# The second block's down projection by Strassen's scheme: seven products of halves, and PSUM banks that are read in the middle of a sum

## The chip, the cores and the metric

The kernel runs on one core of a Trainium2 chip. The metric is the device time of one execution in microseconds, the median of several runs. In one core TensorE (PE in the profile, PEld its weight loads) multiplies, VectorE (DVE) and ScalarE (ACT) work element by element and can read PSUM, the eight banks into which TensorE accumulates, GpSimd (POOL) works element by element on SBUF, and SyncE (SP) starts most of the DMA transfers.

## The reference, cut to what matters

512 tokens of width 1024 go through a first block (a mixer with three branches, cross-attention, a convolutional feed-forward layer) and a second one (two kinds of attention, an output projection, a feed-forward layer). Only the second feed-forward layer bears on the change; its weights are `w_ff1_2` (1024 x 4096) and `w_ff2_2` (4096 x 1024):

```python
D_MODEL, SEQ = 1024, 512
D_FF = 4 * D_MODEL
...
        x = x + merged @ w_out[l]
        h = rms_norm_2(x, g_mlp[l])
        x = x + jnp.square(jax.nn.relu(h @ w_ff1[l])) @ w_ff2[l]
    return rms_norm_2(x, g_final)
```

## The kernel before, in words

**Numbers.** Every fp32 operand of a matrix product is split in two: `h`, a copy rounded to fp32r (ScalarE), and `l`, the rest (VectorE, `l = x - h`). A product is then three matmuls, h·h, h·l and l·h (`mm3`), summed in one PSUM bank. A weight piece is 256 rows by 512 columns or 1024 rows by 128 columns, 512 KB: a DMA brings it into `wr` (four buffers), ScalarE writes `wh` and VectorE `wl` (in this layer four buffers of each, two in the pool `w` and two more in `w_mlp`).

**The layer.** `ffn_relu2` takes the 4096 hidden features in four passes of 1024. In a pass, `gemm_f` (up) makes eight tiles of 128 features by 512 tokens: each is 8 steps of the sum times three matmuls of 512 columns into one bank. `ev_up` takes the bank out as relu times itself into `r` (L468, L469) and splits it into `ah` and `al`. Then `gemm_w` (down) takes two column halves of 512 outputs; for each, four banks hold the four groups of 128 tokens (t), and four weight pieces pass by, each used by all four t: per pass 2 halves x 4 t x 8 steps x 3 matmuls, all of 512 columns. The banks are added to the residual `h` in SBUF (`add_to`, L1527). In the last pass and half, `hold=3` keeps three pieces back, so that the four t end one after the other; `Residual.ev` adds the bank (L346), squares and sums the row on ScalarE (L271), and `step` runs the final norm of the rows behind it: `scale` on GpSimd (L279, L366, L371), `row` on VectorE into `xnt` and a DMA to the output (L387, L389).

**Before the layer.** The output projection (`mh`, `ml` in the pool `mh2`) ends with another `Residual` (`n_mlp`), whose `row` writes `xnt` and whose `turn` transposes it on TensorE into the layer's input `xh`, `xl`. The first two up tiles of the layer run in halves of 256 tokens, so that they can begin before the last two groups of tokens are there.

**Order.** The framework puts in the waits, and it sets the order of the instructions on each engine when the program is built: the context is opened with `schedule_with_timeline_sim=True`, so the order on an engine is one of planned times and not that of the code. On the chip an engine then keeps that order. A tile's buffer is given to the next tile of its name when all that read it are done.

Of the kernel before, what the change touches and what calls it, by code (L numbers as in the profile page):

```python
# [88 lines left out]
class Core:  # L89
# [58 lines left out]
    def wpiece(self, *srcs, pool=False):  # L148
# [9 lines left out]
        for s in srcs:  # L158
            self.nc.sync.dma_start(raw[:, :, c:c + s.shape[1]], s.rearrange("(k p) n -> p k n", p=128))
            c += s.shape[1]  # L160
        self.wi = (self.wi + 1) % (2 + self.wmore)
        p = self.wp if self.wi < 2 else self.wx
# [14 lines left out]

    def mm3(self, out, lh, ll, rh, rl, first, last):
        mm = self.nc.tensor.matmul
        mm(out, lh, rh, start=first, stop=False)  # L180
        mm(out, lh, rl, start=False, stop=False)  # L181
        mm(out, ll, rh, start=False, stop=last)  # L182

# [56 lines left out]
    def gemm_w(self, src, nk, n, xh, xl, evac, hold=1):  # L240
# [10 lines left out]
        for c0 in range(0, n, 512):  # L251
# [9 lines left out]
            for t in range(nt):  # L261
# [3 lines left out]
                yield  # L265


    def sumsq(self, src, ss, out=None):
# [61 lines left out]
class Residual:  # L330
# [3 lines left out]

    def __init__(self, core, pool, h, g, g2=None, dst=None):
        self.core, self.pool, self.h, self.dst = core, pool, h, dst
        self.gb = core.bcast(pool, g, D, "gb")
        self.gb2 = None if g2 is None else core.bcast(pool, g2, D, "gb2")
        self.ss = pool.tile([128, NT, 2, 2], F32, name="rss")
        self.sq = pool.tile([128, 512], mybir.dt.bfloat16, name="rsq")  # L340
        self.wait, self.rs = {}, {}

    def ev(self, t, c0, w, ps):
# [4 lines left out]
        if self.gb2 is not None:  # L348
            nc.gpsimd.tensor_tensor(x, x, self.gb[:, c0:c0 + w], op=ALU.mult)
            self.core.sumsq(x, self.ss[:, t, 1, c0 // 512:c0 // 512 + 1], self.sq)  # L350
        if c0 + w == D:
            self.step(t)

    def step(self, t):
# [18 lines left out]
    def row(self, t):  # L373
# [4 lines left out]
        h, rs = self.h[:, t], self.rs[t]  # L378
        y = self.pool.tile([128, D], F32, name="xnt", bufs=2)
        out = None if self.dst is None else self.dst[t * 128:(t + 1) * 128]  # L380
# [75 lines left out]


def ffn_relu2(core, pool, h, xh, xl, up, down, mid, res):
    nc = core.nc
    nf = down.shape[0] // 128  # L460
    for f0 in range(0, nf, 8):
        n = min(8, nf - f0)
        ah = pool.tile([128, 8, T], F32R, name="ah", bufs=2)
        al = pool.tile([128, 8, T], F32R, name="al", bufs=2)

        def ev_up(m, ps):
            r = pool.tile([128, T], F32, name="r", bufs=3)
            nc.scalar.activation(r, ps, AF.Relu)  # L468
            nc.vector.tensor_tensor(r, ps, r, op=ALU.mult)  # L469
            core.split(ah[:, m], al[:, m], r)  # L470

        yield from core.gemm_f(up[:, f0 * 128:(f0 + n) * 128], 8, n * 128, xh, xl, ev_up, mid if f0 == 0 else None, wide=True)

        yield from core.gemm_w(down[f0 * 128:(f0 + n) * 128], n, D, ah[:, 0:n], al[:, 0:n], *((add_to(core, h),) if f0 + n < nf else (res.ev, 3)))

# [1229 lines left out]
def second_block(core, I, out):  # L1705
# [4 lines left out]
    with ExitStack() as right:  # L1710
# [39 lines left out]
        hp = core.hp.enter_context(core.pool("h2"))  # L1750
        h = hp.tile([128, NT, D], F32, name="h")
        n_mlp = ExitStack()
        with core.weights(1, "w_out2", 2), core.pool("mh2") as p:
# [3 lines left out]
            right.close()  # L1757
            res = Residual(core, n_mlp.enter_context(core.pool("n_mlp", side=1)), h, I["g_mlp_2"])
            drain(core.gemm_w(I["w_out_2"], 8, D, mh, ml, res.ev, 2))
    with core.weights(2, "w_mlp"), core.pool("mlp") as p:  # L1760
        last = Residual(core, p, h, I["g_final_2"], dst=out)

        def mid():
            res.rest()
            n_mlp.close()

        drain(ffn_relu2(core, p, h, *res.x, I["w_ff1_2"], I["w_ff2_2"], mid, last))
        last.rest()
# [46 lines left out]
```

## Time and profile before

| what | value |
|---|---|
| median of 3 runs | 2014.29 us (2011.59 to 2017.02) |
| the profiled execution's own time | 2016.94 us |
| its span, first to last instruction | 2015.1 us |
| TensorE busy | 1958.1 us of the span, 10844 matmuls |
| VectorE busy | 1115.8 us |
| ScalarE busy | 850.8 us |
| granted TensorE clock, mean | 0.983 of full speed |

Busy times are sums of recorded durations. Matmuls overlap in the pipeline, so the record of one (0.39 us) is longer than the distance to the next. The profiled execution took 2.65 us more than the median of the runs; 1.84 us of it lie outside the span.

### The profile page before, as it was taken

The page shows a single profiled execution, that of the slowest core. Times are in us where ns is not written, and L with a number is a line of the kernel's source. Part 1 is how long each engine was busy: PE and PEld are TensorE (multiplying, and loading weights), DVE is VectorE, ACT ScalarE, POOL GpSimd, SP SyncE. Part 2 cuts the span into 40 slices and gives each one's busy share as a digit, 9 for nine tenths or more (in the row PEclk, how much of TensorE's full clock was granted, in tenths as well). Part 3 has the DMA queues.
Part 4 walks back from the last instruction along what each step waited for, and adds up shares of the span by engine and source line. Part 5 has one row for each costly group of instructions (what it writes and reads, how often), then busy time and mean ns, then how long its engine had stood idle before and what let it go on. Part 6 is the DMA issues. An engine that isn't in the chain of part 4 may idle for free.

```text
span 2015.1 us, 27841 instructions
## 1 busy us (share of the span) xinstructions
PE 1958.1 (97%) x10844; PEld 1642.5 (82%) x10844; DVE 1115.8 (55%) x1835; ACT 850.8 (42%) x1474; POOL 321.5 (16%) x367
## 2 busy tenths in 40 slices
PE   7999999999899999999999998999999999999998
PEld 6777888888778988888888877888888878888886
DVE  4457353418965645465454547657889754343343
ACT  4433223335624443343342446567776433233232
POOL 1334123443320100200000021002344020000000
PEclk9999989999999999999999998999999999999999
DMA  6223223342365641333333326442222533333331
GB/s 170 74 68 81 74 76 100 105 151 63 106 226 161 192 125 43 97 104 97 100 96 94 94 87 202 129 126 74 64 80 89 188 105 94 96 96 102 94 94 53
DMA packets 280727, 215.01 MB, mean 107 GB/s; under 512 B 28206, under 2 KB 239812, under 8 KB 280468
## 3 DMA queue, kind: packets, MB, share of 16 engines
q1 hardware_dynamic: 261364, 205.23, 33.9%
q10 hardware_dynamic: 19232, 8.02, 1.6%
q8 instruction: 85, 1.39, 0.3%
q14 instruction: 46, 0.38, 0.1%
HBM read 195.35 MB, written 20.48 MB: 107 GB/s over the span
## 4 chain that ended last, share of the span: by engine, by line
PE 88%; DVE 6%; ACT 2%; issue 2%; POOL 1%; DMA 1%; SPq 1%; ACTq 0%; DVEq 0%; POOLq 0%
PE g L180 17%; PE g L181 16%; PE g L182 16%; PE s L180 9%; PE s L182 9%; PE s L181 9%; PE s L608 1%; PE s L622 1%; PE s L304 1%; PE p L891 1%; DVE sbr L692 1%; PE s L596 1%; PE s L595 1%; DVE ptl L172 1%; DMA wr<-in_ca_wkv_dram 1%
## 5 line engine op out<-in xcount | busy, mean ns | idle before, releaser
L164 ACT ACTIVATE wh<-wr 128x1024 fp32r<-128x1024 f32 x307 | 323.6, 1056 | 585.7 <-PE g L181 192.4
L165 DVE TENSOR_TENSOR wl<-wr,wh 128x1024 fp32r<-128x1024 f32 (+1 forms) x240 | 295.0, 1231 | 417.0 <-ACT wh L164 413.1
L180 PE MATMUL g<-xh,wh 128*128 128x512 f32 (+1 forms) x1168 | 454.7, 391 | 6.1 <-DVE rkr L782 2.4
L181 PE MATMUL g<-xl,wh 128*128 128x512 f32 (+1 forms) x1168 | 452.2, 388 | 2.2 <-DVE xl L172 2.1
L182 PE MATMUL g<-xh,wl 128*128 128x512 f32 (+1 forms) x1168 | 451.1, 387 | 0.0
L180 PEld LDWEIGHTS g<-xh,wh 128*128 128x128 f32 x1168 | 225.2, 193 | 50.9 <-issue 3.7
L181 PEld LDWEIGHTS g<-xl,wh 128*128 128x128 f32 x1168 | 225.4, 193 | 44.0 <-DVE xl L172 3.2
L182 PEld LDWEIGHTS g<-xh,wl 128*128 128x128 f32 x1168 | 225.1, 193 | 42.8 <-DVE wl L165 1.0
L165 POOL TENSOR_TENSOR wl<-wr,wh 128x1024 fp32r<-128x1024 f32 x67 | 169.3, 2530 | 425.3 <-ACT wh L164 410.6
L182 PE MATMUL s<-wh,al 128*128 128x512 f32 x324 | 127.1, 392 | 0.0
L181 PE MATMUL s<-wl,ah 128*128 128x512 f32 x324 | 127.1, 392 | 0.0
L180 PE MATMUL s<-wh,ah 128*128 128x512 f32 x324 | 127.0, 392 | 0.0
L181 PE MATMUL s<-xl,wh 128*128 128x512 f32 x288 | 112.9, 392 | 0.0
L180 PE MATMUL s<-xh,wh 128*128 128x512 f32 x288 | 112.8, 392 | 0.0
L182 PE MATMUL s<-xh,wl 128*128 128x512 f32 x288 | 112.8, 392 | 0.0
L279 POOL TENSOR_TENSOR ss<-rss 128x1 f32<-128x1 f32 (+1 forms) x20 | 6.8, 341 | 468.9 <-ACT rsq L271 468.9
L1122 POOL TENSOR_SCALAR sy<-sy,rsm,ngate 128x128 f32<-128x128 f32 (+1 forms) x64 | 42.5, 666 | 198.5 <-DVE rsm L1120 182.9
L172 DVE TENSOR_TENSOR ptl<-s,pth 128x256 fp32r<-128x256 f32 (+3 forms) x144 | 66.7, 475 | 12.1 <-ACT pth L171 11.2
L181 PEld LDWEIGHTS s<-wl,ah 128*128 128x128 f32 x324 | 60.8, 188 | 14.0
L180 PEld LDWEIGHTS s<-wh,ah 128*128 128x128 f32 x324 | 60.8, 188 | 13.9
L182 PEld LDWEIGHTS s<-wh,al 128*128 128x128 f32 x324 | 60.8, 188 | 14.0
L1118 ACT ACTIVATE sy<-sy,m 128x128 f32<-128x128 f32 (+1 forms) x96 | 53.7, 560 | 39.1 <-DVE m L1116 36.9
(491 smaller groups left out, 3690.7 us busy)
## 6 DMA issues: line engine op xcount, KB each, us to landing
wr<-in_w_ff_dram SPq DMA_DIRECT2D x64, 512.0 KB
wr<-in_w_comb_dram SPq DMA_DIRECT2D x62, 512.0 KB
wr<-in_ffn_up_dram SPq DMA_DIRECT2D x44, 512.0 KB
wr<-in_w_in_dram SPq DMA_DIRECT2D x36, 512.0 KB
wr<-in_ffn_down_dram SPq DMA_DIRECT2D x22, 512.0 KB
wr<-in_ca_wkv_dram SPq DMA_DIRECT2D x16, 512.0 KB
d_gate<-ff SPq DMA_DIRECT2D x24, 256.0 KB
gi<-d_gate SPq DMA_DIRECT2D x24, 256.0 KB
```

Source lines behind the costliest of these rows:

```text
L164: self.nc.scalar.activation(h, raw, AF.Copy)
L165: (self.nc.gpsimd if pool or self.lpool else self.nc.vector).tensor_tensor(l, raw, h.bitcast(F32), op=ALU.subtract)
L172: nc.vector.tensor_tensor(l, src, h.bitcast(F32), op=ALU.subtract)
L180: mm(out, lh, rh, start=first, stop=False)
L181: mm(out, lh, rl, start=False, stop=False)
L182: mm(out, ll, rh, start=False, stop=last)
L304: nc.tensor.transpose(ps[:, j * 128:(j + 1) * 128], x[:, j * 128:(j + 1) * 128], self.ident)
L595: mm(s, q[:, qs], kk[0][:, 0:n], start=True, stop=False)
L596: mm(s, q[:, qs], kk[1][:, 0:n], start=False, stop=last)
L608: core.nc.tensor.transpose(ps[:, c], p[:, c], core.ident)
L1118: nc.scalar.activation(y, y, AF.Exp, scale=-1.0, bias=m, accum_out=sm)
L1122: nc.gpsimd.tensor_scalar(y, y, scalar1=rs, scalar2=fac, op0=ALU.mult, op1=ALU.mult)
```

## The change

The hidden activations A of a pass (512 tokens x 1024 features) are cut into four quarters of 256 tokens x 512 features, the down weights B (1024 x 1024) into four quarters of 512 x 512, and the product is made from seven products of quarters or of their sums and differences (the form with fifteen additions, after Strassen and Winograd). A class `Halves` makes S3 = A11 - A21, S1 = A21 + A22, S2 = S1 - A11 and S4 = A12 - S2 beside A11, A12 and A22 as the up tiles come out of PSUM, and splits all of them. `gemm_s` loads B's quarters into `ws` (left columns) and `wr` (right columns), subtracts quarters in place on VectorE (`less`), splits each for its product, and runs the products. Two pairs of banks, `b1` and `b2`, are read into `h` and then added to by a later product (`more=True` leaves out the framework's check of groups). The normed rows `xnt` of both norms now lie in `ws` in place of two buffers of their own, and `Residual.ev` counts columns to see when a row is full. Blank lines are left out:

```diff
--- before.py
+++ after.py
@@ -158,6 +158,15 @@
         for s in srcs:
             self.nc.sync.dma_start(raw[:, :, c:c + s.shape[1]], s.rearrange("(k p) n -> p k n", p=128))
             c += s.shape[1]
+        return self.wsplit(raw, pool)
+    def wsplit(self, raw, pool=False):
+        k, n = raw.shape[1:]
+        def view(t):
+            return t[:, 0:k * n].rearrange("p (k n) -> p k n", k=k)
         self.wi = (self.wi + 1) % (2 + self.wmore)
         p = self.wp if self.wi < 2 else self.wx
         h, l = (view(p.tile([128, 1024], F32R, name=x)) for x in ("wh", "wl"))
@@ -175,11 +184,14 @@
             nc.vector.scalar_tensor_tensor(l, src, scale, h.bitcast(F32), op0=ALU.mult, op1=ALU.subtract)
-    def mm3(self, out, lh, ll, rh, rl, first, last):
-        mm = self.nc.tensor.matmul
-        mm(out, lh, rh, start=first, stop=False)
-        mm(out, lh, rl, start=False, stop=False)
-        mm(out, ll, rh, start=False, stop=last)
+    def mm3(self, out, lh, ll, rh, rl, first, last, more=False):
+        def mm(l, r, start, stop):
+            self.nc.tensor.matmul(out, l, r, start=start, stop=stop, skip_group_check=more)
+        mm(lh, rh, first, False)
+        mm(lh, rl, False, False)
+        mm(ll, rh, False, last)
     def gemm_f(self, src, nk, n, xh, xl, evac, halves=None, pieces=(), wide=False):
@@ -264,6 +276,68 @@
                 evac(t, c0, 512, pss[t])
                 yield
+    def gemm_s(self, src, ops, evac):
+        nc = self.nc
+        K = src.shape[0] // 2
+        cuts = [(k, min(2, K // 128 - k)) for k in range(0, K // 128, 2)]
+        own = {}
+        def load(i, j):
+            own[i, j] = []
+            for k, m in cuts:
+                p, name = (self.ws, "ws") if j == 0 else (self.wp, "wr")
+                t = p.tile([128, 1024], F32, name=name, bufs=4)[:, 0:m * 512].rearrange("p (k n) -> p k n", k=m)
+                r0 = i * K + k * 128
+                nc.sync.dma_start(t, src[r0:r0 + m * 128, j * 512:j * 512 + 512].rearrange("(k p) n -> p k n", p=128))
+                own[i, j].append(t)
+        def less(dst, a, b):
+            for d, x, y in zip(own[dst], own[a], own[b]):
+                nc.vector.tensor_tensor(d, x, y, op=ALU.subtract)
+        def product(bank, name, b, first, *outs):
+            ws = [self.wsplit(t) for t in own[b]]
+            ah, al = ops[name]
+            for u in range(2):
+                us = slice(u * 128, (u + 1) * 128)
+                for (k0, m), (wh, wl) in zip(cuts, ws):
+                    for k in range(m):
+                        self.mm3(bank[u], ah[:, k0 + k, us], al[:, k0 + k, us], wh[:, k], wl[:, k], first and k0 + k == 0, k0 + k == K // 128 - 1, more=True)
+                for i, j, end in outs:
+                    evac(2 * i + u, 512 * j, bank[u], end)
+        b1 = [self.sbank() for _ in range(2)]
+        load(0, 0)
+        load(1, 0)
+        load(0, 1)
+        product(b1, "A11", (0, 0), True, (0, 0, False))
+        less((0, 0), (0, 1), (0, 0))
+        load(1, 1)
+        yield
+        product([self.gbank() for _ in range(2)], "A12", (1, 0), True, (0, 0, True))
+        yield
+        b2 = [self.sbank() for _ in range(2)]
+        product(b2, "S1", (0, 0), True, (1, 1, False))
+        less((0, 0), (1, 1), (0, 0))
+        yield
+        product(b1, "S2", (0, 0), False, (0, 1, False))
+        yield
+        product(b2, "S4", (1, 1), False, (0, 1, True))
+        less((0, 1), (1, 1), (0, 1))
+        less((1, 0), (1, 0), (0, 0))
+        yield
+        product(b1, "S3", (0, 1), False, (1, 1, True))
+        yield
+        product(b1, "A22", (1, 0), False, (1, 0, True))
+        yield
     def sumsq(self, src, ss, out=None):
         if out is None:
@@ -332,13 +406,13 @@
-    def __init__(self, core, pool, h, g, g2=None, dst=None):
-        self.core, self.pool, self.h, self.dst = core, pool, h, dst
+    def __init__(self, core, pool, h, g, g2=None, dst=None, rows=None):
+        self.core, self.pool, self.h, self.dst, self.rows = core, pool, h, dst, rows
         self.gb = core.bcast(pool, g, D, "gb")
         self.gb2 = None if g2 is None else core.bcast(pool, g2, D, "gb2")
         self.ss = pool.tile([128, NT, 2, 2], F32, name="rss")
         self.sq = pool.tile([128, 512], mybir.dt.bfloat16, name="rsq")
-        self.wait, self.rs = {}, {}
+        self.wait, self.rs, self.seen = {}, {}, [0] * NT
     def ev(self, t, c0, w, ps):
         nc, h = self.core.nc, self.h
@@ -348,8 +422,15 @@
         if self.gb2 is not None:
             nc.gpsimd.tensor_tensor(x, x, self.gb[:, c0:c0 + w], op=ALU.mult)
             self.core.sumsq(x, self.ss[:, t, 1, c0 // 512:c0 // 512 + 1], self.sq)
-        if c0 + w == D:
+        self.seen[t] += w
+        if self.seen[t] == D:
             self.step(t)
+    def ev_s(self, t, c0, ps, last):
+        if last:
+            self.ev(t, c0, 512, ps)
+        else:
+            add_to(self.core, self.h)(t, c0, 512, ps)
     def step(self, t):
@@ -376,7 +457,7 @@
         if t == 0 and not last:
             self.x = core.xn_tiles()
         h, rs = self.h[:, t], self.rs[t]
-        y = self.pool.tile([128, D], F32, name="xnt", bufs=2)
+        y = self.pool.tile([128, D], F32, name="xnt", bufs=2) if self.rows is None else self.rows.tile([128, D], F32, name="ws", bufs=4)
         out = None if self.dst is None else self.dst[t * 128:(t + 1) * 128]
         if self.gb2 is not None:
             nc.vector.scalar_tensor_tensor(y, h, rs[:, 1:2], self.gb2, op0=ALU.mult, op1=ALU.mult)
@@ -455,23 +536,59 @@
         yield from core.gemm_w(down[f0 * 128:(f0 + n) * 128], n, D, ah[:, 0:n], al[:, 0:n], *((add_to(core, h),) if f0 + n < nf else (res.ev, 2)))
+class Halves:
+    def __init__(self, core, pool):
+        self.core, self.pool = core, pool
+    def open(self, n):
+        self.n = n // 2
+        a, b = ([self.pool.tile([128, m, 4, 256], F32R, name=f"a{x}{m}") for x in "hl"] for m in (2, 5))
+        self.parts = a, b
+        self.ops = {nm: [x[:, i, 0:self.n] for x in p] for p, nms in ((a, ("A11", "S3")), (b, ("A12", "A22", "S1", "S2", "S4")))
+                    for i, nm in enumerate(nms)}
+        self.raw = {}
+    def room(self, m):
+        if m < self.n:
+            self.raw[m] = self.pool.tile([128, 3, 256], F32, name="r3", bufs=4)
+            return self.raw[m][:, 0::2]
+        self.raw[m] = self.pool.tile([128, 5, 256], F32, name="r5", bufs=2)
+        return self.raw[m][:, 0:2]
+    def put(self, m):
+        add = self.core.nc.vector.tensor_tensor
+        r, j = self.raw[m], m % self.n
+        if m < self.n:
+            add(r[:, 1], r[:, 0], r[:, 2], op=ALU.subtract)
+            self.core.split(*(x[:, :, j] for x in self.parts[0]), r[:, 0:2])
+        else:
+            q = self.raw.pop(j)
+            add(r[:, 2], q[:, 2], r[:, 1], op=ALU.add)
+            add(r[:, 3], r[:, 2], q[:, 0], op=ALU.subtract)
+            add(r[:, 4], r[:, 0], r[:, 3], op=ALU.subtract)
+            self.core.split(*(x[:, :, j] for x in self.parts[1]), r)
 def ffn_relu2(core, pool, h, xh, xl, up, down, mid, res):
     nc = core.nc
     nf = down.shape[0] // 128
+    a = Halves(core, pool)
     for f0 in range(0, nf, 8):
-        n = min(8, nf - f0)
-        ah = pool.tile([128, 8, T], F32R, name="ah", bufs=2)
-        al = pool.tile([128, 8, T], F32R, name="al", bufs=2)
+        a.open(8)
         def ev_up(m, ps):
-            r = pool.tile([128, T], F32, name="r", bufs=3)
+            r, ps = a.room(m), ps.rearrange("p (u t) -> p u t", u=2)
             nc.scalar.activation(r, ps, AF.Relu)
             nc.vector.tensor_tensor(r, ps, r, op=ALU.mult)
-            core.split(ah[:, m], al[:, m], r)
-
-        yield from core.gemm_f(up[:, f0 * 128:(f0 + n) * 128], 8, n * 128, xh, xl, ev_up, mid if f0 == 0 else None, wide=True)
-
-        yield from core.gemm_w(down[f0 * 128:(f0 + n) * 128], n, D, ah[:, 0:n], al[:, 0:n], *((add_to(core, h),) if f0 + n < nf else (res.ev, 3)))
+            a.put(m)
+        yield from core.gemm_f(up[:, f0 * 128:(f0 + 8) * 128], 8, 1024, xh, xl, ev_up, mid if f0 == 0 else None, wide=True)
+        yield from core.gemm_s(down[f0 * 128:(f0 + 8) * 128], a.ops, res.ev_s if f0 + 8 == nf else lambda t, c0, ps, last: add_to(core, h)(t, c0, 512, ps))
@@ -1749,16 +1866,17 @@
             drain(fox_attend(core, tp, core.fox, 1, fh, fl), branch(core, mp, I["w_br_nsa_2"], nh, nl, d_gb, acc, True))
         hp = core.hp.enter_context(core.pool("h2"))
         h = hp.tile([128, NT, D], F32, name="h")
+        core.ws = core.hp.enter_context(core.pool("ws"))
         n_mlp = ExitStack()
         with core.weights(1, "w_out2", 2), core.pool("mh2") as p:
             mh, ml = (p.tile([128, 8, T], F32R, name=n) for n in ("mh", "ml"))
             drain(branch(core, mp, I["w_br_fox_2"], fh, fl, d_ga, acc, False, (mh, ml)))
             nc.sync.dma_start(h, core.d_h)
             right.close()
-            res = Residual(core, n_mlp.enter_context(core.pool("n_mlp", side=1)), h, I["g_mlp_2"])
+            res = Residual(core, n_mlp.enter_context(core.pool("n_mlp", side=1)), h, I["g_mlp_2"], rows=core.ws)
             drain(core.gemm_w(I["w_out_2"], 8, D, mh, ml, res.ev, 2))
     with core.weights(2, "w_mlp"), core.pool("mlp") as p:
-        last = Residual(core, p, h, I["g_final_2"], dst=out)
+        last = Residual(core, p, h, I["g_final_2"], dst=out, rows=core.ws)
         def mid():
             res.rest()
```

## Rows read from the trace of the kernel before

**Rows 1.** The page, part 1: busy time of each engine.

```profile
PE 1958.1 (97%) x10844; PEld 1642.5 (82%) x10844; DVE 1115.8 (55%) x1835; ACT 850.8 (42%) x1474; POOL 321.5 (16%) x367
```

**Rows 2.** Windows, an up stage, a down stage, sum: PE, PEld, DVE, ACT, POOL; clock.

```profile
1741.00:1784.00 43.00, 43.00 (x188) 35.09 (x187) 19.33 (x23) 15.67 (x21) 0.00 (x0) 1.00 0.32 97
1784.00:1829.00 45.00, 45.00 (x197) 36.78 (x197) 15.73 (x18) 10.24 (x11) 0.00 (x0) 1.00 0.32 94
...
sum 358.00, PE 357.54 PEld 293.90 DVE 143.97 ACT 106.24 POOL 4.56; mean PE 44.69 PEld 36.74 DVE 18.00 ACT 13.28 POOL 0.57
```

**Rows 3.** Timeline of TensorE: first matmul of passes 2 and 4; the last.

```profile
1742.60 0.40 PE L180 MATMUL g<-xh,wh 128*128 128x512 f32 x1
...
1919.27 0.40 PE L180 MATMUL g<-xh,wh 128*128 128x512 f32 x1
...
2007.39 0.40 PE L182 MATMUL s<-wh,al 128*128 128x512 f32 x1
```

**Rows 4.** Groups by shape, VectorE, then ScalarE, 1650 to 2008 us.

```profile
L165 DVE TENSOR_TENSOR wl<-wr,wh 128x1024 fp32r<-128x1024 f32 x60 | 73.5, 1225 | 164.1 <-ACT wh L164 164.1
L172 DVE TENSOR_TENSOR al<-r,ah 128x512 fp32r<-128x512 f32 x32 | 22.2, 692 | 21.1 <-ACT ah L171 21.0
L1527 DVE TENSOR_TENSOR h<-s,h 128x512 f32<-128x512 f32 x18 | 12.1, 688 | 8.2 <-PE s L182 8.2
L469 DVE TENSOR_TENSOR r<-g,r 128x512 f32<-128x512 f32 x17 | 11.6, 684 | 0.0
...
L164 ACT ACTIVATE wh<-wr 128x1024 fp32r<-128x1024 f32 x60 | 63.6, 1061 | 180.0 <-PE s L182 90.1 <-PE g L181 36.1 <-PE s L181 28.0
L171 ACT ACTIVATE ah<-r 128x512 fp32r<-128x512 f32 x32 | 20.2, 633 | 43.3 <-DVE r L469 43.3
```

**Rows 5.** Groups by shape, VectorE, whole span: SBUF sources of 256 and 1024.

```profile
L693 DVE TENSOR_TENSOR sba<-sba,sbr 128x256 f32<-128x256 f32 x8 | 3.3, 418 | 0.4
...
L879 DVE TENSOR_TENSOR rkr<-rkr,re 128x1024 f32<-128x1024 f32 x2 | 2.4, 1212 | 0.0
```

**Rows 6.** Timeline around the start of pass 2; 1748.20 begins its second up tile.

```profile
1738.29 1.23 DVE L165 TENSOR_TENSOR wl<-wr,wh 128x1024 fp32r<-128x1024 f32 x1 [4.37 <-ACT wh L164]
1739.44 1.28 DVE L1527 TENSOR_TENSOR h<-s,h 128x512 f32<-128x512 f32 x2
...
1748.20 0.40 PE L180 MATMUL s<-xh,wh 128*128 128x512 f32 x1
...
1749.13 0.58 ACT L468 ACTIVATE r<-g 128x512 f32<-128x512 f32 x1
...
1749.26 1.23 DVE L165 TENSOR_TENSOR wl<-wr,wh 128x1024 fp32r<-128x1024 f32 x1 [4.14 <-ACT wh L164]
...
1750.40 0.68 DVE L469 TENSOR_TENSOR r<-g,r 128x512 f32<-128x512 f32 x1
```

**Rows 7.** Waits of SP's queue, 1660 to 2008 us: total, times, longest.

```profile
SPq L159 <- DVE wl L165: 289.5, 56, 15.3
```

**Rows 8.** Timeline at the join of output projection and layer, VectorE.

```profile
1643.34 1.23 DVE L165 TENSOR_TENSOR wl<-wr,wh 128x1024 fp32r<-128x1024 f32 x1
...
1644.48 0.68 DVE L346 TENSOR_TENSOR h<-s,h 128x512 f32<-128x512 f32 x1
```

**Rows 9.** Windows of 10 us over the same join.

```profile
1640.00:1650.00 10.00, 6.63 (x38) 5.71 (x37) 8.52 (x8) 7.23 (x14) 8.34 (x8) 0.88 0.27 73
1650.00:1660.00 10.00, 9.75 (x64) 9.21 (x62) 4.17 (x7) 2.12 (x4) 1.76 (x4) 0.78 0.30 86
```

**Rows 10.** Timeline of VectorE at the end.

```profile
2003.65 0.69 DVE L346 TENSOR_TENSOR h<-s,h 128x512 f32<-128x512 f32 x1
2006.38 1.41 DVE L387 SCALAR_TENSOR_TENSOR xnt<-h,rrs,gb 128x512 f32<-128x512 f32 x2 [2.03 <-POOL rrs L371]
2007.82 0.69 DVE L346 TENSOR_TENSOR h<-s,h 128x512 f32<-128x512 f32 x1
2010.55 1.42 DVE L387 SCALAR_TENSOR_TENSOR xnt<-h,rrs,gb 128x512 f32<-128x512 f32 x2 [2.03 <-POOL rrs L371]
```

## The prediction

> **What bounds the kernel now.** The page first: TensorE is busy for 97% of the span, VectorE for 55%, ScalarE for 42% [rows 1]. Since matmul records overlap, I look next at the layer itself, in windows. In an up stage and the down stage behind it TensorE is busy for every microsecond at clock 1.00, VectorE for 19.33 of 43 us and 15.73 of 45 us; over the whole layer, 1650 to 2008 us, TensorE lacks 0.46 us of 358 and VectorE works 144 us [rows 2]. So the layer lasts as long as its matmuls do. The timeline of TensorE gives their distance: pass 2 begins at 1742.60, pass 4 at 1919.27, and its last matmul at 2007.39 [rows 3]. A pass has 192 matmuls up and 192 down, so (1919.27 - 1742.60) / 768 = 0.2300 us each; the record of 0.40 us is not the price, but its end, 0.17 after the next may start, is when a bank can be read.
>
> **What is removed.** A down stage is now 7 products x 2 banks x 4 steps x 3 = 168 matmuls of the same 512 columns, 24 fewer, and four passes make 96 fewer: 96 x 0.2300 = 22.1 us. A product lasts 24 x 0.230 = 5.52 us, a bank's half of it 2.76, the stage 38.6 in place of 44.2.
>
> **What is added on VectorE.** Before, a pass has 16 `wl`, 8 squares, 8 `al` and 8 additions to `h`: 16 x 1.225 + 8 x 0.684 + 8 x 0.692 + 8 x 0.688 = 36.1 us [rows 4]. After it has 22 `wl` (8 up, 14 down; B's quarters are split anew after each `less`), 8 squares, 14 additions to `h`, 8 `less` of 1024, 4 + 12 additions of 256 for the S, 4 `al` of 512 and 4 of 1280. For `less` I take 1.22 and for an addition of 256 0.418, which the scan's and the attention's rows of those sizes show [rows 5]; the 1280 has no row, and from 0.692 at 512 and 1.225 at 1024 the line goes to 1.49. Sum: 26.95 + 5.47 + 9.63 + 9.76 + 6.69 + 2.77 + 5.96 = 67.2 us in a pass of 360 x 0.230 = 82.8. That is 81%, so on average it is covered by TensorE; without that cover the 31 us more in each of four passes would dwarf the gain.
>
> The average isn't the stage. While the seven products run (38.6 us) VectorE has 14 `wl` (the last three are already for the next up tiles), 8 `less`, 14 additions, and the last up tile's square, S and `al` of 3.4 us: 17.2 + 9.8 + 9.6 + 3.4 = 40.0 us by durations. But instructions with no wait between them start closer than they last: a `wl` at 1738.29 is followed after 1.15 us, one at 1749.26 after 1.14, two additions take 1.28 together [rows 6]. By these distances it is 22 x 1.145 + 14 x 0.64 + 3.2 = 37.4 us. The stage is all but full on VectorE.
>
> [...]
>
> Some of this can go early. The first `less` needs only the first product's split and the right-hand quarter; four `wh` buffers let a split run a product ahead, and the up stage (about 30 us of VectorE work in 44 us) has room. Laid out at these distances, the next product's split (2.29), a `less` (2.29) and two additions (1.28) ask for 5.9 us in products 2, 3, 5 and 6, and without a `less` 3.6 in product 4, against 5.52 each, with some 2 us done before. Nothing has to stall, but the reserve is 1 to 3 us a pass.
>
> **The one join that has no slack.** Product 2 needs the parts of the last up tile. In the rows the relu of a tile begins 0.9 us after the next tile's first matmul (1748.20; 1749.13) and its square ends at 1751.08, 2.9 us after it [rows 6]; the split follows. Now three dependent additions (1.25), a copy of 1280 (ScalarE: 0.633 at 512, 1.061 at 1024 [rows 4], so about 1.28) and 1.49 follow: ready at 2.9 + 1.25 + 1.28 + 1.49 = 6.9 us. Product 2 starts at 5.5 and reaches that part at its tenth matmul, 7.6. If the framework takes the strided write as covering all parts, it waits 1.4 us; with a bank's addition in between, 2.0. Bounds 0 to 3 a pass. With the tight VectorE I take 1.0 a pass for both together, 4 us; bounds 0 to 12.
>
> **Banks read between products.** An addition to `h` lasts 0.69. `b1` is read after product 1 and written again by 4; `b2` after 3, written by 5; `b1` after 4, written by 6: a whole product lies between. Only 6 to 7 follow directly, and there bank 0 has 2.76 us for a read that takes 0.17 + 0.69. Nothing, as long as VectorE isn't over 1.9 us late; what is late next would be product 7's bank 1.
>
> **ScalarE** gets 6 more `wh` and the larger `ah`: 22 x 1.061 + 8 x 0.58 [rows 6] + 4 x 0.633 + 4 x 1.28 = 36 us of 82.8. Nothing.
>
> **DMA and SP.** The bytes and the count of 512 KB issues stay (8 up, 8 down a pass). SP's queue waits now for a free `wr` 56 times, 289.5 us [rows 7]: loads are early by the depth of the ring, and no wait of ScalarE is put down to a DMA [rows 4]. After, the right-hand quarters hold all four `wr` from deep in the up stage until `less` and split around products 5 and 6, near 22 to 28 us; SP holds the next pass's up loads behind them. The first must be split by 38.6 - 2.3 = 36.3 us. A load at full rate (94 GB/s at a share of 0.32 [rows 2], so 294) is 1.8 us. Nothing; if that cover goes, a load or two per pass, 6 to 15 us in all.
>
> **Join and tail.** `xnt` in four buffers and 16 KB of shift: nothing; the join idles 3.4 us now [rows 9], so -2 to +2. At the end, token group 2 finishes 2.76 us before the last, no longer 4.17 (rows of addition 2003.65 and 2007.82). Its `xnt` comes 2.73 us after its addition and lasts 1.41 [rows 10], so now it falls on the last addition, which may start up to 1.4 us late. I take 0.7.
>
> **Sum.** 2016.94 - 22.1 + 4 + 0.7 = 1999.5 for the profiled execution, and 2.65 less, 1996.9, for the median of runs: 1997. Its own bounds: nothing lost and runs 2 us faster, 1990; 12 + 1.4 lost, 2006.
>
> **Rivals.** (a) *Late operands inside the passes*: VectorE behind by more than its reserve, or the next up loads late: 6 to 15 us more come back, 2003 to 2009. For it: 37.4 to 40.0 of 38.6 us. Against: work that can be done ahead. Chance 0.16. (b) *Slower: VectorE takes things in the order of the code.* Then a product's `less` and split stand behind the addition that waits for the end of the product before. At 3 to 4: 0.17 + 0.69 + 3 x 1.225 = 4.5 us idle; at 5 to 6, with four `less`, 7.0. Over 5.5 us a pass it is a loss; here 11.5 x 4 = 46, so 2016.9 - 2.65 - 22.1 + 46 = 2038, and 2072 if the other four joins wait 0.86 + 1.225 = 2.1 each too. Against: the order isn't the code's; a `wl` of the layer runs before the last addition of the projection ahead of it [rows 8]. Chance 0.11. (c) *The clock falls.* [...] Chance 0.06. (d) *It doesn't do what it says*: the count of matmuls doesn't fall by 96; the code's loops leave no room for it. 0.01.
>
> **Numbers.** The forecast has 0.64; 0.02 is left for times under 1990. A measurement of this kernel tells 0.3% (6 us) from no change, so faster means under 2008.2 and slower over 2020.3. Faster: 0.64 + 0.02 + most of (a) = 0.80. Slower: (b) and a part of (c), 0.13. Same: 0.07. The range 1990 to 2011 takes in the forecast's bounds and (a), and leaves out (b) and (c).
>
> **What would show it.** Right: 96 fewer matmuls at 0.230, TensorE idle under 4 us in passes 2 to 4, VectorE near 67 us a pass, no wait of TensorE for `h`. The join: TensorE waiting for `al` at the second product. Wrong: waits of TensorE on `wl` behind a `less`, an addition to `h` ahead of them in VectorE's order, or a granted clock under 1.00 in a down stage.

## The result, and the profile after

The changed kernel takes 1997.38 us (median of 4 runs, 1990.71 to 1998.17); the kernel before, run beside it, takes 2015.14 (4 runs, 2011.59 to 2017.02). The ratio is 0.9907, 95% interval 0.9881 to 0.9932. The forecast was 1997, range 1990 to 2011. The profiled execution took 1998.17 us with a span of 1996.4, where the sum had said 1999.5. An agreement within 0.4 us is in part luck: the four runs spread over 7.5 us, and the same kernel, run again later, took 1995.04.

The page's busy times, as in [rows 1]:

```profile
PE 1937.1 (97%) x10748; PEld 1625.0 (81%) x10748; DVE 1227.7 (61%) x1979; ACT 884.3 (44%) x1498; POOL 322.3 (16%) x367
```

There are 96 matmuls fewer than before, and VectorE works 112 us more (busy time counts overlapping records once; by the sum of its durations after 1650 us it is 125 us, 31 a pass as forecast); TensorE's share stays at 97%. The windows of the layer, as in [rows 2], first from product 1 of one pass to product 1 of the next, three times, then the end of the layer:

```profile
core 0: us, PE busy (x) PEld busy (x) DVE busy (x) ACT busy (x) POOL busy (x), PEclk, DMA share, GB/s
1699.31:1782.10 82.79, 82.79 (x362) 67.63 (x360) 63.64 (x78) 34.30 (x40) 0.00 (x0) 1.00 0.34 102
1782.10:1865.03 82.93, 82.93 (x361) 67.62 (x360) 62.98 (x77) 34.30 (x39) 0.00 (x0) 1.00 0.35 102
1865.03:1947.81 82.78, 82.78 (x361) 67.66 (x360) 63.40 (x77) 34.30 (x39) 0.00 (x0) 1.00 0.34 102
...
1950.00:1992.00 42.00, 36.96 (x160) 29.52 (x158) 33.82 (x42) 17.49 (x29) 4.93 (x12) 0.97 0.10 38
```

A pass lasts 82.8 us, 360 matmuls by 0.230, with TensorE busy for all of it at clock 1.00: nothing of the four times 1.0 us put down for late operands was lost there. All that TensorE waits for from 1650 to 1995 us stands in its waits (us in total, times, longest):

```profile
PE s L190 <- DVE h L420: 0.8, 1, 0.8
PE g L190 <- ACT xh L180: 0.3, 1, 0.3
```

The first is in the last pass, ahead of product 7; the second is in the first up tile, where the kernel before has the like. Such rows give idle time between records. As a matmul's record (0.39) outlasts the distance to the next (0.230) by 0.16, a stop costs TensorE 0.16 us more than its row says: 0.96 us for the 0.80 of the first. VectorE's groups by shape, as in [rows 4], agree with the sum's durations; the copy of 1280 that had no row takes 1.487 us where 1.49 was put down:

```profile
L174 DVE TENSOR_TENSOR wl<-ws,wh 128x1024 fp32r<-128x1024 f32 x40 | 48.9, 1222 | 13.0 <-ACT wh L173 12.7
...
L181 DVE TENSOR_TENSOR al<-r,ah 128x1280 fp32r<-128x1280 f32 x16 | 23.8, 1487 | 0.3
L303 DVE TENSOR_TENSOR ws<-wr,ws 128x1024 f32<-128x1024 f32 x16 | 19.5, 1216 | 0.0
```

Yet the operand that the prediction worried about came far later than it said. VectorE's timeline from the square of the last up tile of pass 2, and then ScalarE's copy `ah` of the same tile; product 1 begins at 1865.03:

```profile
1869.38 0.68 DVE L587 TENSOR_TENSOR r<-g,r 128x512 f32<-128x512 f32 x1
1870.41 1.23 DVE L174 TENSOR_TENSOR wl<-ws,wh 128x1024 fp32r<-128x1024 f32 x1 [0.35 <-ACT wh L173]
...
1872.15 0.42 DVE L571 TENSOR_TENSOR r<-r,r 128x256 f32<-128x256 f32 x1
1872.49 1.22 DVE L174 TENSOR_TENSOR wl<-ws,wh 128x1024 fp32r<-128x1024 f32 x1
1873.62 1.22 DVE L303 TENSOR_TENSOR ws<-wr,ws 128x1024 f32<-128x1024 f32 x1
1874.76 0.42 DVE L572 TENSOR_TENSOR r<-r,r 128x256 f32<-128x256 f32 x1
...
1877.36 0.42 DVE L573 TENSOR_TENSOR r<-r 128x256 f32<-128x256 f32 x1
...
1881.11 1.49 DVE L181 TENSOR_TENSOR al<-r,ah 128x1280 fp32r<-128x1280 f32 x1
```

```profile
1878.87 1.26 ACT L180 ACTIVATE ah<-r 128x1280 fp32r<-128x1280 f32 x1
```

The square (L587), the three short additions (L571 to L573) and the split of five parts (L181) are a chain; the planned order puts a `less` (L303) or a `wl` into every step of it, so `al` begins 16.1 us after product 1 and not after 5.4. The parts are there after 15.1 (`ah`) and 17.6 us (`al`), where the prediction had 6.9. TensorE doesn't wait because its own order isn't that of the products either. Its timeline of the same stage (a tile named `s` is a bank of products 1, 3, 4 to 7 or of every second up stretch, `g` one of product 2 or of an up stretch; `xh` marks an up tile):

```profile
1865.03 0.39 PE L190 MATMUL s<-wh,ah 128*128 128x512 f32 x1
...
1870.47 0.40 PE L190 MATMUL g<-wh,ah 128*128 128x512 f32 x1
...
1872.57 0.63 PE L190 MATMUL s<-wh,ah 128*128 128x512 f32 x2
1873.04 0.40 PE L190 MATMUL g<-wh,ah 128*128 128x512 f32 x1
...
1898.24 0.40 PE L190 MATMUL g<-xh,wh 128*128 128x512 f32 x1
...
1903.26 0.39 PE L190 MATMUL s<-wh,ah 128*128 128x512 f32 x1
```

Product 2 is cut up: 9 matmuls of its first bank, 2 of the next product, 9 of its second bank, then 28 more of the products behind it before the first that needs the last tile. By the code product 3 has only 18 that can do without this tile, so of these 2 + 28 = 30 the other 12 are product 4's. And before product 7 (1903.26) stand 22 matmuls of the next pass's first up tile, so that bank 0 of product 6 has 5 us more to be read.

**The ledger.** From the first up matmul to the last of the layer: before 1650.31 to 2007.39, 357.08 us; after 1651.10 to 1987.36, 336.26. That is 20.8 less, where 22.1 was the price of the matmuls: 0.96 came back ahead of product 7 in the last pass, 0.3 is not assigned. The end behind the last matmul grew from 7.7 to 9.0, 1.3 (0.7 forecast). The layer began 0.8 later, and additions of the output projection ahead of the join were late by as much (1639.27 before, 1640.05 after), so the join is unchanged. -20.8 + 1.3 + 0.8 = -18.7, the change of the span (2015.1 to 1996.4). Against the sum that is 3.0 less for late operands (4 put down, 0.96 measured), 0.6 more behind the last matmul, 0.8 more at the layer's start and the 0.3: in all 1.3 less, 1998.2 in place of 1999.5.

The layer's start is no property of the change. In the profile of the changed kernel run again (the last experiment has its times) the layer begins at 1643.73 in place of 1651.10, and then lasts 336.37 us against 336.26. The instructions ahead of it are the same, in the same order on each engine, but the granted clock differs, here from 220 to 310 us, first in this run and then in the other:

```profile
220.00:310.00 90.00, 90.00 (x930) 74.88 (x929) 38.63 (x77) 23.44 (x37) 18.90 (x9) 0.91 0.29 76
220.00:310.00 90.00, 88.89 (x968) 73.51 (x967) 41.86 (x82) 25.64 (x40) 21.12 (x10) 0.96 0.28 75
```

Why it differs is not shown. A difference of some 7 us between two executions can lie ahead of the layer, so the experiments are read by the layer and the pass, and only then by the total.

The end of the profile, VectorE's order:

```profile
1979.78 1.41 DVE L468 SCALAR_TENSOR_TENSOR ws<-h,rrs,gb 128x512 f32<-128x512 f32 x2
1981.11 0.68 DVE L420 TENSOR_TENSOR h<-s,h 128x512 f32<-128x512 f32 x1
...
1987.73 1.42 DVE L468 SCALAR_TENSOR_TENSOR ws<-h,rrs,gb 128x512 f32<-128x512 f32 x2 [2.03 <-POOL rrs L452]
1989.06 0.68 DVE L420 TENSOR_TENSOR h<-s,h 128x512 f32<-128x512 f32 x1
```

Twice a row of the final norm (1.41 us) stands ahead of an addition: at 1979.78 ahead of the one that frees bank 0 for product 7, at 1987.73 ahead of the very last one.

### The profile page after: what moved, and what is told of

Same layout as the page of the kernel before. It is cut to its first block, busy times and chain, and to the rows that moved or that the text cites. A ratio compares the mean times of both kernels' runs of the same rounds, so it can differ in the third digit from the quotient of the medians.

```text
span 1996.4 us, 27818 instructions
## 1 busy us (share of the span) xinstructions
PE 1937.1 (97%) x10748; PEld 1625.0 (81%) x10748; DVE 1227.7 (61%) x1979; ACT 884.3 (44%) x1498; POOL 322.3 (16%) x367
## 4 chain that ended last, share of the span: by engine, by line
PE 88%; DVE 6%; ACT 3%; issue 2%; POOL 1%; SPq 0%; DMA 0%; ACTq 0%; DVEq 0%; POOLq 0%
PE g L190 49%; PE s L190 27%; PE s L725 1%; PE s L739 1%; PE s L378 1%; PE p L1008 1%; DVE sbr L809 1%; PE s L713 1%; PE s L712 1%; DVE ptl L181 1%; PE o L1138 0%; PE s L1144 0%; SPq L1718 0%; PE s L1393 0%; DVE sba L810 0%
## 5 line engine op out<-in xcount | busy, mean ns | idle before, releaser
L173 ACT ACTIVATE wh<-wr 128x1024 fp32r<-128x1024 f32 x291 | 305.8, 1055 | 470.4 <-PE g L190 202.4
L174 DVE TENSOR_TENSOR wl<-wr,wh 128x1024 fp32r<-128x1024 f32 (+1 forms) x224 | 274.9, 1230 | 280.7 <-ACT wh L173 276.2
L173 ACT ACTIVATE wh<-ws 128x1024 fp32r<-128x1024 f32 x40 | 42.4, 1061 | 76.2 <-PE s L190 44.3
L181 DVE TENSOR_TENSOR ptl<-s,pth 128x256 fp32r<-128x256 f32 (+3 forms) x144 | 66.7, 475 | 12.2 <-ACT pth L180 11.2
L190 PEld LDWEIGHTS s<-wh,ah 128*128 128x128 f32 x324 | 60.8, 188 | 15.1 <-issue 1.2
```

Of the source, the lines that this page charges most:

```text
L173: self.nc.scalar.activation(h, raw, AF.Copy)
L174: (self.nc.gpsimd if pool or self.lpool else self.nc.vector).tensor_tensor(l, raw, h.bitcast(F32), op=ALU.subtract)
L181: nc.vector.tensor_tensor(l, src, h.bitcast(F32), op=ALU.subtract)
L190: self.nc.tensor.matmul(out, l, r, start=start, stop=stop, skip_group_check=more)
```

## Experiments

Each ratio is against the kernel before, run on the same chip in turn; the medians of before were 2015.4 to 2016.2. In all of them "pass period" is the time from product 1 of a pass to product 1 of the next in the middle of the layer, 82.9 in the changed kernel.

**1. An eighth product.** Product 2 is computed twice, the second time over the first, and evacuated once.

```diff
-            for u in range(2):
+            for u, _ in ((u, i) for u in range(2) for i in range(2 if name == "A12" else 1)):
...
-                for i, j, end in outs:
+                for i, j, end in outs if _ or name != "A12" else ():
```

> Product 2 is computed twice into its banks, so a down stage has eight products (192 matmuls) again, while VectorE, ScalarE and the loads stay as in the changed kernel. Theory A (the time is the count of matmuls at 0.230 us, all other work is covered): 96 x 0.230 = 22.1 us come back, 2017 to 2020 us, up to 1 us less where the waits of the last pass get shorter. Rival B (the gain comes from the new loads, buffers or order and not from the matmuls): within 3 us of the changed kernel's 1997.4.

2027.99 us (2027.2 to 2028.58), ratio 1.0062 [1.0047, 1.0078], 30.6 over the changed kernel. 22.1 of that are the matmuls; the period grew by 7.4, of which 5.5 are matmuls and 1.3 a gap in product 2, where TensorE waits for the last tile:

```profile
PE g L190 <- ACT ah L180: 4.6, 4, 1.2
```

So the matmuls carry the gain at their full price, and with eight products the scheme would be slower than the plain loop. The size was missed by 8 us: 5.2 of it are these gaps (four, with 0.16 each). The layer itself grew by 28.5 us (336.26 to 364.76), 22.1 + 5.2 and 1.2 that is not assigned; the other 2 lie outside it.

**2. TensorE held to the order of the products.** The matmuls of each bank are issued behind the last one before them.

```diff
-            self.nc.tensor.matmul(out, l, r, ...)
+            self.mm = self.nc.tensor.matmul(out, l, r, ...)
...
+            last = self.mm
...
+                with self.tc.issue_after(last.ins):
+                    for (k0, m), (wh, wl) in zip(cuts, ws):
...
+                last = self.mm
```

> The seven products run on TensorE strictly one bank after the other in the order of the code; in the changed kernel the order interleaves products 2 and 3 (runs of 9, 2, 9, 28 and 4 matmuls change between the banks) and VectorE finished the last up tile's al 16.1 us after product 1 began (1865.03 and 1881.11), long after product 2 had begun. Theory A (the interleaving is what hides the late last up tile): TensorE waits in product 2 of each pass, by the prediction's figure for that join 1.4 to 2.0 us (6 to 8 us in all), by the trace after up to 10 us a pass (2005 to 2037 us). Rival B (VectorE's order moves with TensorE's and nothing is late): at most 2 us, 1997 to 1999.

2030.17 us (2026.76 to 2033.03), ratio 1.0073 [1.0053, 1.0092]: the whole gain is gone. Waits of TensorE, and its windows around one of them:

```profile
PE g L190 <- ACT ah L180: 25.7, 4, 6.5
PE g L190 <- DVE al L181: 1.2, 4, 0.3
```

```profile
1700.00:1707.00 7.00, 0.75 (x4) 0.27 (x2) 7.00 (x9) 1.02 (x1) 0.00 (x0) 0.76 0.00 0
1707.00:1712.00 5.00, 4.39 (x10) 3.00 (x11) 2.27 (x3) 0.25 (x1) 0.00 (x0) 0.50 0.00 0
1712.00:1717.00 5.00, 5.00 (x19) 4.04 (x18) 3.07 (x3) 2.11 (x2) 0.00 (x0) 0.81 0.26 71
```

In every pass product 2 stops at its tenth matmul for 6.4 to 6.5 us, and once more for 0.3: the place that the prediction named, with the last tile's parts 14.2 (`ah`) and 15.7 us (`al`) after product 1 in place of 6.9. VectorE is busy through the stop. Behind it the granted clock is 0.50 for the next 5 us and 0.81 for 5 more, 5 x 0.50 + 5 x 0.19 = 3.4 us of full speed. The stops, 7 us a pass with 0.16 for each, and the clock together are about the 9.8 us by which the period grew (92.70). The layer grew by 37.9 us (336.26 to 374.12). The total shows less of it because the layer began 6.3 us earlier in this execution (1644.80), with the same order on every engine ahead of it; that lies within what the unedited kernel shows.

**3. VectorE in the order of the code** (the rival for slower): `less` and the splits of products 2 to 7 stand behind the last addition to `h`.

```diff
             for d, x, y in zip(own[dst], own[a], own[b]):
-                nc.vector.tensor_tensor(d, x, y, op=ALU.subtract)
+                with self.tc.issue_after(self.add.ins):
+                    nc.vector.tensor_tensor(d, x, y, op=ALU.subtract)
...
-            ws = [self.wsplit(t) for t in own[b]]
+            with self.tc.issue_after(self.add.ins) if name != "A11" else ExitStack():
+                ws = [self.wsplit(t) for t in own[b]]
...
```

> On VectorE each less and each split of a product is put behind the last addition to h of the product before (as in the order of the code); nothing else changes. Theory A (the prediction's rival b: then less and split stand between two products): 4.5 us idle before product 4 and 7.0 before product 6, 11.5 a pass, 2038 to 2043 us, up to 2075 where the other four joins wait 2.1 us each; a few us less where the next pass's first up tile fills one join. Rival B (VectorE's order does not matter, since it has 15 us to spare in a pass): under 2005 us.

2099.43 us (2095.28 to 2104.9), ratio 1.0419 [1.0393, 1.0444]. Waits of TensorE in the layer and two windows:

```profile
PE s L190 <- DVE wl L174: 30.0, 17, 2.7
PE s L190 <- ACT wh L173: 29.6, 12, 3.1
PE s L190 <- DVE h L1646: 2.2, 4, 0.6
```

```profile
1812.00:1822.00 10.00, 7.61 (x27) 5.88 (x27) 6.20 (x7) 0.12 (x1) 0.00 (x0) 0.84 0.00 0
...
1852.00:1862.00 10.00, 7.86 (x24) 6.28 (x25) 4.90 (x5) 3.31 (x4) 0.00 (x0) 0.66 0.99 292
```

All waits come to 63.4 us, 15.9 a pass (17 with 0.16 for each stop), between the 11.5 and the 19.9 that the rival had priced. But the period grew by 26.2: in six windows of 10 us from about the first stop the clock was .97 .84 .84 .84 .83 .66, which is at most another 10.2 us, as TensorE stood still in part of that time. The mechanism is right, and its price was low by the clock.

**4. How much more VectorE work fits.** Some `wl` are computed twice: 2, 4 or 7 a pass (one of the two of products 3 and 5; of 2 to 5; of all). At 1.14 us from start to start that is 2.3, 4.6 and 8.0 us.

The edit with two; the others differ in the names:

```diff
+        for _ in range(2 if more else 1):
+            (...).tensor_tensor(l, raw, h.bitcast(F32), op=ALU.subtract)
...
-            ws = [self.wsplit(t) for t in own[b]]
+            ws = [self.wsplit(t, more=i == 0 and name in ("S1", "S4")) for i, t in enumerate(own[b])]
```

> The wl of the first weight piece of each of the seven products is computed twice: 7 x 1.145 = 8.0 us more on VectorE in each pass, on its busiest stretch. Theory A (the prediction's reserve of 1 to 3 us in a down stage): 5 to 7 us of each pass show, 2017 to 2025 us. Rival B (the whole pass is the reserve, 67.2 of 82.8 us, since work moves between up and down stages): 75.2 of 82.8 fits, under 2003 us.

> As in the run with seven doubled wl, but only two (first piece of the products with S1 and S4): 2.3 us more on VectorE in a pass. Theory A (the reserve of a down stage is 1 to 3 us): 0 to 1.3 us of each pass show, 1995 to 2001 us. Rival B (there is no reserve, the changed kernel only just fits): all 2.3 show, and the clock falls behind the waits as it did with seven: over 2004 us.

> Four doubled wl (products with A12, S1, S2, S4), 4.6 us more on VectorE in a pass. Theory A: 1.6 to 3.6 us of each pass show, 2002 to 2012 us. Rival B (the cost is proportional from the start): near 4/7 of the 28 us that seven cost, 2010 to 2014 us. Rival C (the knee is later): under 2001 us.

| `wl` doubled | VectorE work added a pass | median | ratio [95%] | pass period, growth |
|---|---|---|---|---|
| 2 | 2.3 | 2007.01 (2002.57 to 2008.63) | 0.9956 [0.9940, 0.9972] | 85.09, 2.2 |
| 4 | 4.6 | 2022.39 (2015.76 to 2025.41) | 1.0032 [1.0019, 1.0045] | 89.33, 6.4 |
| 7 | 8.0 | 2023.70 (2020.87 to 2027.81) | 1.0041 [1.0021, 1.0060] | 90.21, 7.3 |

With two, the whole 2.3 us shows; the clock stays at 1.00. The waits of TensorE:

```profile
PE s L191 <- DVE h L1645: 2.8, 4, 0.7
PE g L191 <- ACT ah L181: 1.6, 4, 0.4
PE s L191 <- ACT wh L173: 0.9, 4, 0.2
```

So there was no reserve here, where the prediction had 1 to 3 us a pass. The planner's order had moved in this run too (behind product 2's second nine matmuls come 18 of other products where there were 28), so this holds for the work with the order planned for it. With four, all expectations missed: more came back than was added. The waits show why, and a window behind the longest of them:

```profile
PE s L191 <- DVE h L1645: 8.7, 3, 2.9
PE s L191 <- DVE wl L175: 6.3, 8, 2.2
```

```profile
1800.00:1805.00 5.00, 4.06 (x9) 2.88 (x10) 5.00 (x6) 0.00 (x0) 0.00 (x0) 0.69 0.37 108
```

A bank that is read between its products now is late, by 2.9 us, and the clock falls to 0.69 behind it. The planned order had changed more (products 2 to 6 are cut up in another way), so how much of it is the work and how much the order stays open. With seven, within its expectation, it is the place of experiment 2 again: TensorE waits 9.1 us for the last tile's `ah` and 5.3 for its `al`, up to 3.3 at once, and the clock is 0.62 from 1806 to 1812 us.

**5. Products in order, `less` behind the last tile.** Experiment 2, and each `less` is issued behind the `al` of the last up tile, so that the chain isn't interrupted by it.

```diff
+            self.al = nc.vector.tensor_tensor(l, src, h.bitcast(F32), op=ALU.subtract)
...
+                with self.tc.issue_after(self.al.ins):
+                    nc.vector.tensor_tensor(d, x, y, op=ALU.subtract)
...
```

> As in the run with pinned products, TensorE takes the seven products strictly in the order of the code, and in addition VectorE does each less only behind the al of the pass's last up tile. Theory A (the last up tile was late there, 14.2 us after product 1 began, because six less and splits stood between its short additions; the prediction's 6.9 us is its time when it comes first): the wait in product 2 falls from 6.6 us to under 2 a pass, the clock does not fall, and the time goes from 2030 to 1997 to 2010 us. Rival B (VectorE simply has too much to do at that point): what is taken from product 2's wait comes back before product 3, and the time stays over 2020 us.

2023.74 us (2019.83 to 2026.17), ratio 1.0038 [1.0022, 1.0054]. The parts are there 8.1 (`ah`) and 9.6 us (`al`) after product 1, as the split of the tile before and two additions to `h` still stand between the steps of the chain. Product 2 waits 1.15 us a pass by the rows, 1.5 with 0.16 for each of two stops. The rest comes back one product later:

```profile
PE s L190 <- DVE wl L174: 16.7, 16, 1.7
PE g L190 <- DVE al L181: 3.2, 4, 0.8
PE g L190 <- ACT ah L180: 1.4, 4, 0.4
```

The chain's last step in pass 2 (product 1 begins at 1787.82):

```profile
1795.96 1.49 DVE L181 TENSOR_TENSOR al<-r,ah 128x1280 fp32r<-128x1280 f32 x1 [1.34 <-ACT ah L180]
```

The period is 89.91, 7.0 longer. With the products in order the work is too much between products 1 and 4 in both of VectorE's orders that were tried, this and experiment 2's; in the changed kernel TensorE's own order hides it. The clock is 1.00 in all of this layer: 24 stops, none over 1.7 us.

**6. Three `wh` and `wl` in place of four.** `core.weights(2, "w_mlp")` becomes `core.weights(1, "w_mlp")`.

> Three buffers of wh and wl in place of four for the layer. Theory A (four buffers let a split run a whole product ahead of its use, and this is what lets VectorE work without TensorE waiting): the second piece of a product can be split only once three quarters of the product before are through, 1.4 us plus its own first 1.4 us for 2.3 us of ScalarE and VectorE work behind one another, so TensorE waits up to 1 us in each of 28 products, and more in the up stages: 2005 to 2040 us. Rival B (the buffers are not what matters): under 2001 us.

2023.13 us (2017.5 to 2024.26), ratio 1.0031 [1.0018, 1.0045]. The waits are of every kind (`al` 4.1 us, `wh` 3.4, `h` 4.8, `wl` 2.1 in the layer) and short, none over 1.4 us but one of 2.6 ahead of product 7 in the last pass. The up tile no longer stands before product 7 in TensorE's order. In the second pass the clock fell amid such short stops: five between 1799 and 1809 us, of 1.4, 0.7, 0.6, 0.4 and 0.3 us. The longest two in TensorE's waits from 1795 to 1815 us, and a window:

```profile
PE g L190 <- DVE al L181: 1.4, 1, 1.4
PE s L190 <- ACT wh L173: 0.7, 1, 0.7
...
```

```profile
1805.00:1815.00 10.00, 8.63 (x22) 6.11 (x23) 4.85 (x7) 1.28 (x3) 0.00 (x0) 0.66 0.50 159
```

In the first and the last pass the matmuls behind the same five waits were 0.23 us apart, as at 1.00, and 0.43 in the second. Four buffers are needed; whether by the splits that run a product ahead or by the order that is planned with them, this run doesn't separate.

**7. The tail.** The rows of the final norm are issued behind the additions of products 6 and 7.

```diff
-            self.step(t)
+            if self.dst is not None and self.rows is not None:
+                self.scale(t)
+                self.queue.append(t)
+            else:
+                self.step(t)
...
+        if t > 1 and self.queue and self.queue[0] != t:
+            with self.core.tc.issue_after(self.core.add.ins):
+                self.row(self.queue.pop(0))
...
-        last.rest()
+        last.row(3)
```

> In the last pass the final norm's rows 0 and 1 are put behind the additions of product 6 on VectorE, and row 2 behind the last addition. Theory A (two places where VectorE's order makes something on the path wait: 0.96 us before product 7 of the last pass, where a row's 1.4 us stood ahead of an addition, and 1.33 us before the last addition): TensorE has no gap before product 7, the time from the last matmul to the end falls from 9.0 to 7.7 us, 2.3 us less in all, about 1995. Rival B (the rows are then late themselves, or the output transfers): no gain, 1997, and the tail stays near 9 us.

Beside it the changed kernel ran again, unedited:

> The changed kernel once more, beside the next one on the same chip. All theories: 1991 to 1999 us.

1994.15 us (1986.3 to 1995.92), ratio 0.9884 [0.9865, 0.9903], against 1995.04 (1990.9 to 1996.59), 0.9900 [0.9883, 0.9916]. VectorE's order at the end:

```profile
1984.59 0.69 DVE L420 TENSOR_TENSOR h<-s,h 128x512 f32<-128x512 f32 x1 [2.10 <-PE s L190]
1985.19 1.41 DVE L475 SCALAR_TENSOR_TENSOR ws<-h,rrs,gb 128x512 f32<-128x512 f32 x2
1987.60 1.41 DVE L475 SCALAR_TENSOR_TENSOR ws<-h,rrs,gb 128x512 f32<-128x512 f32 x2 [1.00 <-POOL rrs L459]
```

The wait before product 7 is gone (first up matmul to last matmul 335.19 us, against 336.37 in the run beside it), and from the last matmul to the end it takes 8.05 in place of 9.0: 2.1 us in the traces. By the times the two cannot be told apart. By its layer and its end it is the fastest version of these; by the total it is not shown to be.

## Why the prediction was right

**Right, with its reason.** *What bounds the kernel, and what is removed.* The period is 360 matmuls by 0.230, and experiment 1 gives the product back at its price and more. *VectorE's durations*: all within 0.01 us. *ScalarE, DMA, join*: no wait put down to them but the 0.3 us in the first up tile, which was there before. *VectorE's distances*: it counted an instruction up to the start of the next and not by its recorded length, and rightly: at 1873.62 `less` starts 1.13 us after a `wl` that lasts 1.22.

**Right in the sum, wrong underneath.** *"With the tight VectorE I take 1.0 a pass for both together, 4 us"* measured 0 in three passes and 0.96 in the last, for another reason. Two errors in it cancelled, and that is luck. *"Ready at 2.9 + 1.25 + 1.28 + 1.49 = 6.9 us"* took the chain as uninterrupted; `al` was there 17.6 us after product 1. The wait of 1.4 to 2.0 that followed from the 6.9 is near experiment 5's 1.5 by chance: there `al` comes after 9.6 us and product 2 stops at its tenth and twelfth matmul, not at its start. *"A reserve of 1 to 3 us"* was about zero in experiment 4, with the order planned there; what VectorE has free, some 19 us of a pass, lies elsewhere: it is idle for 5.4 us before it reads product 7's bank 0 at 1906.18. What the prediction did not see is that the planner reorders TensorE as well: cut up, products 2 to 4 give the late tile the time it needs. Experiment 2 shows what that is worth: 9.8 us a pass, some 7 of stops and the rest by the clock.

**Mis-sized.** *The tail*, 0.7: 1.3 behind the last matmul. The prediction had the cause and the upper bound (a row of 1.41 us on the last addition) and took half of it. *"Banks read between products: nothing, as long as VectorE isn't over 1.9 us late"*: 0.96 in the last pass. There a row stands ahead of the addition and no up tile is left to fill with; in the first three passes the 22 up matmuls hid it. Experiment 7 takes the row away, and the wait goes.

**The rivals.** (b) had the place and the stops right (15.9 us a pass in experiment 3), but priced a stop as if TensorE went on at full speed after it. (c) did not come by itself: between products TensorE stops once, for 0.96 us, and the clock is 1.00 in all three whole passes. Its chance of 0.06, of which a part is in the 0.13 for slower, was the author's estimate. In one pass of experiment 6 the clock fell amid five stops of 0.3 to 1.4 us, to 0.66 over 10 us. In experiment 5, 24 stops of up to 1.7 us, 21.3 us in all, left it at 1.00. The longer stops of experiments 2 to 4 were followed by a lower clock: 6.5 us by 0.50 over 5 us (experiment 2), stops of up to 3.1 us by 0.66 over 10 us at the lowest (experiment 3), 2.9 us by 0.69 over 5 us (experiment 4). In the kernel before, a bank got 24 matmuls at a time in the up stages and 6 in `gemm_w`, at clock 1.00 in both [rows 2]. (a) is what experiments 4 and 6 bring about by a small push: 2.3 us of VectorE work or one buffer less, each with the order that the planner made of it.

**Open:** the 0.3 us of the ledger, how far the work and how far the order makes experiment 4 with four `wl` worse than proportional, and what decides whether short stops lower the clock.

## What to carry to other kernels

A product saved was worth its matmuls by their distance here (22.1 us by the count, 20.8 off the layer), as the added vector work fitted stage by stage; sum such work for the stretch in which it is needed, and don't count time that lies behind the last use as reserve (some 19 us of a pass were free on VectorE, and 2.3 us more still showed in full in experiment 4). Where the order on the engines is planned, read it from the trace before and after: here a short dependent chain on a busy engine was stretched by whatever else was ready (17.6 us in place of 6.9), and independent work on the other engine hid it in the changed kernel and not in experiment 2 (a stop of 6.5 us a pass). Price a stop of TensorE by its length and by the clock behind it (6.5 us, then 3.4 us of full speed, in experiment 2). Where the part that wasn't changed differs from one execution to the next (1651.1 and 1643.7 us to the layer here), compare the part that was (336.3 and 336.4).

## What the runs showed of the hardware

- A stop of 6.5 us was followed by a granted clock of 0.50 over 5 us and 0.81 over the next 5 (experiment 2), one of 2.9 us by 0.69 over 5 us (experiment 4). The length of the longest stop doesn't tell it here: 24 stops of up to 1.7 us, 21.3 us in all, left the clock at 1.00 (experiment 5), while five stops of up to 1.4 us, 3.4 us in all, went with 0.66 over 10 us in one pass of experiment 6 and with matmuls 0.23 us apart, as at 1.00, in two others.
- The same instructions in the same order took 1651.1 us to the layer in one execution and 1643.7 in another, with a granted clock of 0.91 and 0.96 from 220 to 310 us; the layer lasted 336.3 and 336.4.
- A bank that is read between two products and then added to cost TensorE nothing in 15 of the 16 such joins of the four passes, two banks each; one has a wait (0.8 us), where a row of the norm stands ahead of the read.
- VectorE started the next instruction before the recorded end of the last also with the new operations: `less` at 1873.62, 1.13 us after a `wl` that lasts 1.22.
